# Row-wise sums of squares on ScalarE, r on POOL, and key stores on ScalarE's queue, in a diffusion block's first projections

## The chip, the cores and the metric

The kernel runs on one core of a Trainium2 chip. The metric is the device time of one execution in microseconds (us). The engines are TensorE (PE in the profile, PEld for its weight loads), VectorE (DVE), ScalarE (ACT), GpSimd (POOL) and SyncE (SP), which only issues DMAs here. DMAs go out from an engine's own queue: SP's, or ScalarE's.

## The reference

One layer of a block over 2048 latent tokens and 256 context tokens of width 1024. Tokens are normalised, scaled and shifted, projected, mixed, and projected back:

```
r     = rsqrt(mean(x*x, axis=-1) + 1e-6)
h     = x * r * norm_g * (1 + scale) + shift      # scale, shift from silu(c) @ w_ada
q,k,v,gate (two groups of heads) = h @ w_in       # h for latent and for context tokens
y     = neighbourhood attention (+ context keys), two-way retention
out   = rmsnorm(x + gate * (concat(y) @ w_out)) * final_g
```

The change is in the first line, in the order of the work that makes h, and in the queue of one kind of store.

## The kernel before, in words

All matmuls run on 32-bit data split into a high and a low part, three products for each (high by high, low by high, high by low). Tokens come in nine groups of 256: groups 0 to 7 are latent, group 8 is context. Two groups make a block of 512 tokens.

**Making h.** x is loaded transposed (features on partitions) as `raw[i]`, two halves u of four rows of 128 features. For one group i the acts are:
- `sq` (`squares`): ScalarE squares both halves into `st` tiles; POOL (half 0) and VectorE (half 1) add the feature rows, VectorE joins them (L198 to L203).
- `cs` (`colsum`): TensorE sums over the partitions with a column of ones (L209).
- `rs` (`rstd`, `spread_copy`): VectorE makes mean plus eps, POOL takes the power -0.5, VectorE copies r into a 128 by 256 tile (L214, L215, L220).
- `sp` (`spread`): TensorE multiplies that copy with the identity, so r stands along the columns (L227).
- `mu`: VectorE multiplies half u by r (L241). `ab`: VectorE and ScalarE apply scale and shift (L272, L274). `hl`: ScalarE casts the high part, VectorE or POOL subtracts to get the low part (L279, L283).
- `p`: for groups 0 and 1, scale, shift and split of one feature row k (L262 to L265).
- `s`, `m`, `ar`, `af`: the products with w_ada, the copy of their row, and its transposes (L298 to L332). `x` loads a group, `blk` takes buffers.

**The order.** Nothing is scheduled automatically: each engine runs its instructions in the order in which the program emits them. Five key windows, b = 0 to 4, run over the four blocks of latent tokens and the context; each has 32 steps of three matmuls (L363), numbered n = 0 to 159. In window 0 the four units (128 key columns each) are interleaved, later they follow one another. After step n, `run_acts` emits the acts that `PLAN` lists for n (-1 is ahead of window 0). When a unit is done, ScalarE casts it out of PSUM into an `o` tile, VectorE subtracts (L383, L384) and the tile is stored to `kS` through `store`, on the queue `env["queue"]`. There are two `o` buffers and four `st` buffers. `spill_step` stores finished h to `hS` on SP's queue, for later stages.

**Later stages.** The remaining projections (L374, L671) start after window 4, with weights that are loaded to `st`, cast and split (L345, L347); attention, retention and the output projection follow and are not touched.

Of the kernel before, what the change touches and what calls it, by code (L numbers as in the profile page):

```python
# [9 lines left out]
F32 = mybir.dt.float32  # L10
BF16 = mybir.dt.bfloat16
F32R = mybir.dt.float32r
AF = mybir.ActivationFunctionType
# [5 lines left out]
P = 128  # L19
# [39 lines left out]
]  # L59
# [23 lines left out]
def hybrid_kernel(ctx: ExitStack, tc: tile.TileContext, a: dict, out: bass.AP):  # L83
# [46 lines left out]
    KH = KC // 2  # L130
    env = dict(pp=pool(psx, "pp", 6, space=PSUM), st=pool(sx, "st", 4, side="right"), queue=nc.sync)

# [59 lines left out]
    sqs, rms, rbs, prs = {}, {}, {}, {}  # L192

    def squares(i):
        sqs[i] = []
        for u in range(2):
            sq = xsq[i][u] if i < 2 else env["st"].tile([P, KH, 256], F32, name="st")
            nc.scalar.activation(sq, raw[i][u], AF.Square)  # L198
            eng = (nc.gpsimd, nc.vector)[u]
            eng.tensor_tensor(sq[:, 0:2, :], sq[:, 0:2, :], sq[:, 2:4, :], ALU.add)  # L200
            eng.tensor_tensor(sq[:, 0, :], sq[:, 0, :], sq[:, 1, :], ALU.add)
            sqs[i].append(sq)
        nc.vector.tensor_tensor(sqs[i][0][:, 0, :], sqs[i][0][:, 0, :], sqs[i][1][:, 0, :], ALU.add)  # L203

    def colsum(*ii):
        pm = ptile(None if ii[0] < 4 else psm)
        for j, i in enumerate(ii):
# [4 lines left out]
    def rstd(i):  # L212
        r = env["st"].tile([P, 2], F32, name="rs", bufs=4)
        nc.vector.tensor_scalar(r, rms[i], 1.0 / D, EPS, ALU.mult, ALU.add)  # L214
        nc.gpsimd.tensor_tensor(r, r, mhalf[:, 0:2], ALU.pow)  # L215
        rbs[i] = r

    def spread_copy(i):
        rbs[i, 1] = env["st"].tile([P, 2, P], F32, name="t0", bufs=2)
        nc.vector.tensor_copy(rbs[i, 1], rbs[i].unsqueeze(2).to_broadcast([P, 2, P]))  # L220

# [94 lines left out]
    def ada_row(u):  # L316
        rows[u] = op.tile([P, 2, 512], F32, name="o")[:, 0, :]
        n = 4 if SPL[u] else 2
        (nc.scalar.copy, nc.vector.tensor_copy)[u % 2](rows[u][0:n, :], aps[u][0:n, :])

# [144 lines left out]
    for name, *args in LOADS:  # L465
        lds[name](*args)
    acts = dict(sq=squares, cs=lambda *i: colsum(*i), rs=lambda i: (rstd(i), spread_copy(i)), sp=lambda *i: spread(*i),
                mu=lambda i, u: spread_mul(i, (u,)), ab=prep_ab, hl=prep_hl, blk=alloc_blk, x=load_x, w=lambda: wr.append(w_raw(2560)),
# [22 lines left out]
    def window(b):  # L491
        units = [u_k(w01, 512 + 256 * g, ct, b) for g in range(2) for ct in range(2)]
        left = [KC] * 4
        for n, u in enumerate(STEPS if b == 0 else [u for u in range(4) for _ in range(KC)]):
            if b == 4 and n == 0:
                env["queue"] = nc.scalar
            if b == 4 and n % 8 == 0:
# [1127 lines left out]
```

## Time and profile before

| | before |
|---|---|
| median of 3 runs | 1355.98 us (1355.51 to 1357.14) |
| profiled execution | 1356.78 us, of which 1354.9 us are its span |
| mean granted TensorE clock | 0.995 |
| TensorE, VectorE, ScalarE, POOL busy | 97%, 62%, 45%, 43% |
| DMA traffic | 287.26 MB, mean 212 GB/s |

The span runs from the first to the last instruction. A timeline row reads: start, duration, engine, line, operation, out<-in, shapes, count, and in brackets the idle time before it and what ended that. A row of several instructions gives their joint duration. A wait row reads: who waited for whom, us in total, times, longest. In a row of stretches the last three numbers are granted clock, share of the DMA engines that was busy, and GB/s.

### The profile page before, as it was taken

What the parts mean: (1) busy time and instruction counts of PE and PEld (TensorE: products, weight loads), DVE (VectorE), ACT (ScalarE), POOL (GpSimd) and SP (SyncE); (2) the same over time, 40 slices, a digit from 0 to 9 for tenths busy, and PEclk for the clock granted to TensorE, in tenths of its full rate; (3) what the DMA queues carried; (4) which work ended last, traced back from release to release, by engine and by line L of the source; (5) the groups of instructions that cost most, each with busy time, mean ns of one, the idle gap of its engine ahead of it and who ended that gap; (6) DMA issues with size and microseconds to landing.
All of it is one profiled execution on the core that took longest, in us unless ns stands there. A gap on an engine that the chain in (4) does not pass through costs nothing.

```text
span 1354.9 us, 23100 instructions
## 1 busy us (share of the span) xinstructions
PE 1308.3 (97%) x8236; PEld 1148.7 (85%) x8236; DVE 835.2 (62%) x1444; ACT 606.3 (45%) x1259; POOL 579.0 (43%) x569
## 2 busy tenths in 40 slices
PE   6989999999999999999999999999999999999997
PEld 2467899878898888998899889889999789888885
DVE  5786356776666754377767777776654734444445
ACT  5454333243533344455555465556643244333432
POOL 5452102545104664345535474655523164544442
PEclk9999999999999999999999999999999999999999
DMA  9386788564966657967487887766528888445443
GB/s 363 135 279 233 264 293 224 183 220 154 337 184 209 210 188 238 254 199 210 144 225 203 231 225 205 194 181 193 167 86 294 282 300 273 160 156 171 163 134 117
DMA packets 172086, 287.26 MB, mean 212 GB/s; under 512 B 17345, under 2 KB 92225, under 8 KB 170690
## 3 DMA queue, kind: packets, MB, share of 16 engines
q1 hardware_dynamic: 139554, 228.35, 55.5%
q10 hardware_dynamic: 32416, 57.42, 11.8%
q8 instruction: 66, 1.08, 0.3%
q14 instruction: 50, 0.41, 0.1%
HBM read 194.48 MB, written 91.23 MB: 211 GB/s over the span
## 4 chain that ended last, share of the span: by engine, by line
PE 69%; DMA 9%; DVE 7%; POOL 5%; issue 5%; ACT 3%; SPq 1%; ACTq 0%; POOLq 0%; DVEq 0%
PE mm L374 19%; PE mm L1466 11%; PE mm L671 10%; PE mm L363 7%; PE sS L1028 4%; PE tr L1055 3%; PE po L1076 3%; PE mm L1190 2%; PE tr L1057 2%; PE po L1078 2%; DMA st<-in_w_in_dram 2%; DMA kS<-o 1%; DMA v<-rvS 1%; POOL hlo L531 1%; PE mm L1378 1%
## 5 line engine op out<-in xcount | busy, mean ns | idle before, releaser
L374 PE MATMUL mm<-whi,hlo 128*128 128x256 f32 x832 | 229.2, 283 | 2.0 <-DVE hlo L531 2.0
L374 PE MATMUL mm<-whi,hhi 128*128 128x256 f32 x768 | 224.9, 293 | 0.0
L374 PE MATMUL mm<-wlo,hhi 128*128 128x256 f32 x768 | 217.7, 283 | 0.6 <-DVE wlo L347 0.6
L1059 ACT CAST pt<-tr 128x640 fp32r<-128x640 f32 (+1 forms) x128 | 95.6, 747 | 160.8 <-PE tr L1057 158.3
L1065 DVE TENSOR_TENSOR pt<-tr,pt 128x640 fp32r<-128x640 f32 (+1 forms) x128 | 113.9, 890 | 78.2 <-ACT pt L1059 76.9
L374 PEld LDWEIGHTS mm<-whi,hlo 128*128 128x128 f32 x832 | 157.2, 192 | 2.6 <-DVE hlo L531 2.5
L1048 POOL TENSOR_SCALAR sp<-sp,stt 128x640 f32<-128x640 f32 (+2 forms) x128 | 103.2, 809 | 106.4 <-DVE stt L1047 76.0
L374 PEld LDWEIGHTS mm<-wlo,hhi 128*128 128x128 f32 x768 | 146.8, 191 | 0.8 <-DVE wlo L347 0.8
L374 PEld LDWEIGHTS mm<-whi,hhi 128*128 128x128 f32 x768 | 147.1, 191 | 0.1
L625 POOL TENSOR_TENSOR whi<-st,whi 128x512 fp32r<-128x512 f32 x48 | 64.7, 1369 | 163.1 <-ACT whi L624 163.1
L1037 DVE CUSTOM_DVE_ANT_0 sp<-sS,nb 128x640 f32<-128x640 f32 (+2 forms) x128 | 105.5, 824 | 35.7 <-POOL wlo L347 22.9
L1042 ACT ACTIVATE sp<-sp,stt 128x640 f32<-128x640 f32 (+2 forms) x128 | 107.5, 839 | 20.2 <-DVE stt L1037 19.1
L363 PE MATMUL mm<-hlo,whi 128*128 128x512 f32 x256 | 101.7, 397 | 7.3 <-DVE hlo L283 2.3
L363 PE MATMUL mm<-hhi,whi 128*128 128x512 f32 x256 | 108.0, 422 | 0.0
L1028 PE MATMUL sS<-k,q 128*128 128x256 f32 (+3 forms) x512 | 99.3, 316 | 6.4 <-DVE stt L1037 6.2
L363 PE MATMUL mm<-hhi,wlo 128*128 128x512 f32 x256 | 101.7, 397 | 0.3 <-DVE wlo L347 0.3
L671 PE MATMUL mm<-hhi,whi 128*128 128x512 f32 x336 | 97.4, 394 | 0.0
L1466 PE MATMUL mm<-wor,y 128*128 128x512 f32 x384 | 95.7, 398 | 1.2 <-DVE xt L1475 0.9
L1475 DVE TENSOR_TENSOR xt<-mm,xt 128x512 f32<-128x512 f32 x64 | 43.8, 686 | 82.7 <-PE mm L1466 82.6
L1028 PEld LDWEIGHTS sS<-k,q 128*128 128x128 f32 x512 | 82.8, 188 | 13.7 <-DVE stt L1037 9.9
L1466 PE MATMUL mm<-won,y 128*128 128x512 f32 x336 | 89.9, 406 | 0.0
L1466 PEld LDWEIGHTS mm<-wor,y 128*128 128x128 f32 x384 | 69.9, 188 | 17.4 <-issue 3.5
(258 smaller groups left out, 3037.6 us busy)
## 6 DMA issues: line engine op xcount, KB each, us to landing
st<-in_w_in_dram SPq DMA_DIRECT2D x64, 512.0 KB
q<-qS SPq DMA_DIRECT2D x64, 256.0 KB
hlo<-hS SPq DMA_DIRECT2D x20, 512.0 KB
k<-kS SPq DMA_DIRECT2D x16, 576.0 KB
kS<-o SPq DMA_DIRECT2D x16, 512.0 KB
vB<-o SPq DMA_DIRECT2D x64, 128.0 KB
qS<-o ACTq DMA_DIRECT2D x16, 512.0 KB
woS<-g ACTq DMA_DIRECT2D x32, 256.0 KB
```

The costliest lines, as they stand in the source:

```text
L363: nc.tensor.matmul(pm[:, :n], ww[:, k, cs], h[:, k, :], start=(k == 0 and i == 0), stop=(k == KC - 1 and i == 2))
L374: nc.tensor.matmul(pm[:, t * WG:(t + 1) * WG], h[:, k, o:o + P], ww[:, k, :], start=(k == 0 and i == 0), stop=(k == KC - 1 and i == 2))
L625: nc.gpsimd.tensor_tensor(t[:, 1], r, f(t)[:, 0], ALU.subtract)
L671: nc.tensor.matmul(pm, ww[:, k, :], hh[:, k, :], start=(k == 0 and i == 0), stop=(k == KH - 1 and i == 2))
L1028: nc.tensor.matmul(o, hd["q"][i][:, hl, j * P:(j + 1) * P], k, start=(hl == 0), stop=(hl == 1))
L1037: nc.vector.tensor_tensor_reduce(T["sp"][:, :n], T["s"], nbz[big][:, o:o + n], -1.0, 3e38, ALU.add, ALU.min, T["st"][:, 0:1])
L1042: nc.scalar.activation(sp[:, :n], sp[:, :n], AF.Exp, bias=st[:, 0:1], scale=-1.0, accum_out=st[:, 1:2])
L1048: nc.gpsimd.tensor_scalar(sp[:, :n], sp[:, :n], st[:, 2:3], 0.0, ALU.mult, ALU.add)
L1059: nc.scalar.copy(pt[:, :ng_ + 2, 0, :], tr[:, :ng_ + 2, :])
L1065: nc.vector.tensor_tensor(pt[:, :n, 1, :], tr[:, :n, :], f(pt)[:, :n, 0, :], ALU.subtract)
L1466: nc.tensor.matmul(pm, yy[:, k, :], ww[:, k, sl], start=(k == 0 and i == 0), stop=(k == 3 and i == 2))
L1475: nc.vector.tensor_tensor(xts[t][:, sl], pm, xts[t][:, sl], ALU.add)
```

## The change

For groups 2 to 8, x is loaded a second time, untransposed (tokens on partitions, act `xt`, two tiles of 128 tokens), and ScalarE squares a tile in place and sums along its row in the same instruction (`accum_out`). The adds on POOL and VectorE and TensorE's column sums of these groups are gone. POOL makes mean plus eps, the power and the copy. The row copy of modulation column 2 moves from ScalarE to VectorE. Key stores are issued on ScalarE's queue from the first window on, instead of from window 4. `PLAN` is written anew up to window 2.

```diff
 PLAN = [
...
-    (4, 's', 2, 0), (4, 'x', 4), (4, 'p', 2), (5, 'sq', 2), (7, 'm', 2, 0), (8, 'm', 2, 1), (9, 'p', 3),
+    (4, 's', 2, 0), (4, 'x', 4), (4, 'p', 2), (7, 'm', 2, 0), (8, 'm', 2, 1), (9, 'p', 3), (9, 'sq', 2), (9, 'sq', 3),
...
+    (16, 'af', 3), (16, 'xt', 7), (17, 'p', 7), (17, 'rs', 4), (18, 'p', 6), (18, 'hl', 3, 0), (18, 'mu', 3, 1),
...
-    env = dict(pp=pool(psx, "pp", 6, space=PSUM), st=pool(sx, "st", 4, side="right"), queue=nc.sync)
+    env = dict(pp=pool(psx, "pp", 6, space=PSUM), st=pool(sx, "st", 4, side="right"), queue=nc.scalar)
...
+    def load_xt_(i):
+        sqs[i] = []
+        src = a["ctx"] if i == 8 else a["x"][i * 256:(i + 1) * 256, :]
+        for t in range(2):
+            xt = env["st"].tile([P, KH, 256], F32, name="st").rearrange("p k t -> p (k t)")
+            nc.sync.dma_start(xt, src[t * P:(t + 1) * P, :])
+            sqs[i].append(xt)
+
     def squares(i):
+        if i >= 2:
+            rms[i] = env["st"].tile([P, 2], F32, name="rs", bufs=4)
+            for t, xt in enumerate(sqs[i]):
+                nc.scalar.activation(xt, xt, AF.Square, accum_out=rms[i][:, t:t + 1])
+            return
...
     def rstd(i):
-        r = env["st"].tile([P, 2], F32, name="rs", bufs=4)
-        nc.vector.tensor_scalar(r, rms[i], 1.0 / D, EPS, ALU.mult, ALU.add)
+        r = rms[i] if i >= 2 else env["st"].tile([P, 2], F32, name="rs", bufs=4)
+        (nc.gpsimd if i >= 2 else nc.vector).tensor_scalar(r, rms[i], 1.0 / D, EPS, ALU.mult, ALU.add)
         nc.gpsimd.tensor_tensor(r, r, mhalf[:, 0:2], ALU.pow)
...
-        nc.vector.tensor_copy(rbs[i, 1], rbs[i].unsqueeze(2).to_broadcast([P, 2, P]))
+        (nc.gpsimd if i >= 2 else nc.vector).tensor_copy(rbs[i, 1], rbs[i].unsqueeze(2).to_broadcast([P, 2, P]))
...
-        (nc.scalar.copy, nc.vector.tensor_copy)[u % 2](rows[u][0:n, :], aps[u][0:n, :])
+        (nc.scalar.copy, nc.vector.tensor_copy)[u > 0](rows[u][0:n, :], aps[u][0:n, :])
...
-            if b == 4 and n == 0:
-                env["queue"] = nc.scalar
```

New lines shift the numbers: L265 is L278 in the changed kernel, L272 is L285, L279 is L292, L283 is L296, L383 is L396 and L384 is L397; L151 is the store's line in both.

The order on POOL around step 23 of window 0. Before (L200 and L201 add squares, L215 is the power, L265 a low part of `p`, L283 a low part of `hl`):

```order
L200 TENSOR_TENSOR st<-st 128x512
L201 TENSOR_TENSOR st<-st 128x256
L215 TENSOR_TENSOR rs<-rs,mhalf 128x2 x2
L265 TENSOR_TENSOR hlo<-hhi 128x256 x3
L215 TENSOR_TENSOR rs<-rs,mhalf 128x2
L283 TENSOR_TENSOR hlo<-hlo,hhi 128x4x256 x2
```

POOL at the same place now (L227, L228 and L233 are mean plus eps, power and copy of r, here of groups 4 and 5):

```order
L296 TENSOR_TENSOR hlo<-hlo,hhi 128x4x256
L278 TENSOR_TENSOR hlo<-hhi 128x256 x2
L227 TENSOR_SCALAR rs<-rs 128x2
L228 TENSOR_TENSOR rs<-rs,mhalf 128x2
L233 COPY t_501<-rs 128x256
L278 TENSOR_TENSOR hlo<-hhi 128x256
L227 TENSOR_SCALAR rs<-rs 128x2
L228 TENSOR_TENSOR rs<-rs,mhalf 128x2
L233 COPY t_531<-rs 128x256
L296 TENSOR_TENSOR hlo<-hlo,hhi 128x4x256
```

The first low part of group 2 has moved ahead of the last three low parts of `p`, and r of group 4 stands between them.

ScalarE from the end of window 0 to the casts of groups 4 and 5, before (L383 casts a unit, L198 squares, L274 scales, L279 casts a half group):

```order
L383 CAST o<-mm 128x512
L198 ACTIVATE st<-hhi 128x1024 x2
L383 CAST o<-mm 128x512
L274 ACTIVATE hhi<-hhi,mods 128x256 x2
L383 CAST o<-mm 128x512 x2
L274 ACTIVATE hhi<-hhi,mods 128x256 x2
L198 ACTIVATE st<-chi 128x1024 x2
L274 ACTIVATE hhi<-hhi,mods 128x256
L279 CAST hhi<-hhi 128x4x256 x3
```

ScalarE at the same place now (from the third unit of window 0 on; L206 squares with a row sum, L151 issues a key store):

```order
L396 CAST o<-mm 128x512
L151 DMA kS_64<-o 256x1x512
L206 ACTIVATE st,rs<-st 128x1024 x2
L396 CAST o<-mm 128x512
L151 DMA kS_61<-o 256x1x512
L287 ACTIVATE hhi<-hhi,mods 128x256 x2
L206 ACTIVATE st,rs<-st 128x1024 x2
L396 CAST o<-mm 128x512
L151 DMA kS_61<-o 256x1x512
L287 ACTIVATE hhi<-hhi,mods 128x256 x2
L396 CAST o<-mm 128x512
L151 DMA kS_62<-o 256x1x512
```

Behind every cast of a unit now stands the issue of its store, which waits for VectorE's subtraction; the squares that follow are those of later groups.

More of the change, by code (lines that the diff above doesn't have):

```diff
@@ L192, in hybrid_kernel @@
     sqs, rms, rbs, prs = {}, {}, {}, {}
-    def squares(i):
+    def load_xt_(i):
[5 more added lines that the diff above has]
+            sqs[i].append(xt)
+    def squares(i):
+        if i >= 2:
[3 more added lines that the diff above has]
+            return
         sqs[i] = []
         for u in range(2):
-            sq = xsq[i][u] if i < 2 else env["st"].tile([P, KH, 256], F32, name="st")
+            sq = xsq[i][u]
             nc.scalar.activation(sq, raw[i][u], AF.Square)
@@ L205, in colsum @@
     def colsum(*ii):
-        pm = ptile(None if ii[0] < 4 else psm)
+        pm = ptile()
         for j, i in enumerate(ii):
@@ L466, in hybrid_kernel @@
         lds[name](*args)
-    acts = dict(sq=squares, cs=lambda *i: colsum(*i), rs=lambda i: (rstd(i), spread_copy(i)), sp=lambda *i: spread(*i),
+    acts = dict(sq=squares, xt=load_xt_, cs=lambda *i: colsum(*i), rs=lambda i: (rstd(i), spread_copy(i)), sp=lambda *i: spread(*i),
                 mu=lambda i, u: spread_mul(i, (u,)), ab=prep_ab, hl=prep_hl, blk=alloc_blk, x=load_x, w=lambda: wr.append(w_raw(2560)),
```

29 rows, old and new, of the table PLAN are left out of this document.

## The prediction

> **What bounds the kernel now.** I read the page's first lines, then what TensorE waits for up to 240 us, then that stretch's granted clock and DMA share, then the timelines of the engines around each wait.
>
> ```profile
> span 1354.9 us, 23100 instructions
> PE 1308.3 (97%) x8236; PEld 1148.7 (85%) x8236; DVE 835.2 (62%) x1444; ACT 606.3 (45%) x1259; POOL 579.0 (43%) x569
> PE mm L311 <- ACT o L298: 10.3, 1, 10.3
> ...
> PE mm L374 <- DVE wlo L347: 1.3, 2, 0.7
> ```
>
> TensorE is busy 97% of the span, so only its waits and its own work can be won. The change touches the windows of keys and what prepares their activations. Of TensorE's waits up to 240 us, the 10.3 us at the start are untouched. The others, 9.6 us with the rows below, are for low parts of activations (L283, L265), for a spread of r (L227) and for low parts of weights (1.3 us, L347):
>
> ```profile
> 37.85 0.50 PE L363 MATMUL mm<-hlo,whi 128*128 128x512 f32 x1 [1.72 <-DVE hlo L265]
> 59.03 1.38 PE L227 MATMUL mm<-ident,t 128*128 128x128 f32 x8
> 65.12 0.47 PE L363 MATMUL mm<-hlo,whi 128*128 128x512 f32 x1 [0.37 <-DVE hlo L265]
> 74.40 0.47 PE L363 MATMUL mm<-hlo,whi 128*128 128x512 f32 x1 [1.96 <-DVE hlo L283]
> 77.75 0.47 PE L363 MATMUL mm<-hlo,whi 128*128 128x512 f32 x1 [0.38 <-DVE hlo L283]
> 100.83 0.49 PE L363 MATMUL mm<-hlo,whi 128*128 128x512 f32 x1 [2.32 <-POOL hlo L283]
> 104.03 0.50 PE L363 MATMUL mm<-hlo,whi 128*128 128x512 f32 x1
> 106.27 0.88 PE L227 MATMUL mm<-ident,t 128*128 128x128 f32 x4 [1.51 <-DVE t L220]
> ...
> 107.37 0.63 PE L363 MATMUL mm<-hlo,whi 128*128 128x512 f32 x1
> 107.80 0.63 PE L363 MATMUL mm<-hhi,wlo 128*128 128x512 f32 x1
> 104.00:108.00 4.00, 2.47 (x9) 1.84 (x10) 3.04 (x6) 1.10 (x2) 2.67 (x3) 0.84 0.61 208
> ```
>
> Each step n of a window is three matmuls of 0.23 us, 0.69 us. 65.12 is step 23, 74.40 and 77.75 steps 32 and 36, 100.83 and 104.03 steps 64 and 68. After the two waits around 100 and 106 the clock reads 0.84 (last but two columns), and six matmuls come 0.43 us apart instead of 0.23: 1.2 us more.
>
> **What is taken away.** The column sums are seven groups' small matmuls:
>
> ```profile
> 51.87 0.79 PE mm L209 x8
> 109.70 0.58 PE mm L209 x4
> 124.87 0.34 PE mm L209 x4
> 35.49 1.37 DVE L263 TENSOR_SCALAR hhi<-hhi,mods 128x256 f32<-128x256 f32 x1
> 36.90 0.90 DVE L265 TENSOR_TENSOR hlo<-hhi 128x256 fp32r<-128x256 f32 x1
> 28.41 0.40 DVE L263 TENSOR_SCALAR hhi<-hhi,mods 128x256 f32<-128x256 f32 x1
> 35.24 1.47 POOL L200 TENSOR_TENSOR st<-st 128x512 f32<-128x512 f32 x1
> ```
>
> Groups 2 and 3 cost 0.79, group 7 (at the slow clock) 0.58, the other four 0.34 each: 2.7 us of TensorE's own time go (-2.7). The adds of squares on POOL also hold up VectorE: the scaling at 35.49 took 1.37 us beside a POOL add, alone it takes 0.40, and the subtraction behind it took 0.90 where half is usual. TensorE's wait at 37.85 hangs on these two, so 1.4 of its 1.72 us go (-1.4). r of groups 6 and 7 is ready long before its spread, so the wait of 1.51 goes (-1.5).
>
> **Loads.** Fourteen loads of 512 KB (7.3 MB) are added on SP's queue.
>
> ```profile
> 50.00:60.00 10.00, 10.00 (x41) 4.76 (x40) 7.84 (x17) 2.67 (x5) 5.13 (x6) 1.00 0.00 1
> 31.93 4.10 SPq L190 DMA_DIRECT2D hhi<-in_xT_dram  x4
> SPq L151 <- DVE o L384: 79.6, 14, 33.3
> ```
>
> The DMA engines stand idle there (0.00 in the last column but one) because SP, after 36 us, waits 33.3 us at the first key store. Six of the seven groups' loads go into that hole. The first four take the places at 31.93 that groups 4 and 5 had; those then come some 5 us later and are needed only at step 26. Cost: nothing, since the hole covers it; without it a load would cost about 1 us, what each of the four at 31.93 took to get into the full queue. The copy of row 2 of the modulation moves from ScalarE to VectorE, which then has nothing else ready: nothing.
>
> **Step 23, a new wait.** Spread 2 and 3 come at step 14 instead of 16. With the savings, two steps and four transposes less before them they start near 55 us (59.03 before). VectorE then does two multiplications (1.2 us each) and four scalings (0.35), and ScalarE casts group 2 by 60.0. POOL does, in this order, group 2's first low part, two of p 7, r of group 4, and only then the low part of p 6 that step 23 needs.
>
> ```profile
> 60.45 1.22 DVE L241 TENSOR_TENSOR hlo<-hlo,mm 128x1024 f32<-128x1024 f32 x1 [0.53 <-PE mm L227]
> 69.59 2.41 POOL L283 TENSOR_TENSOR hlo<-hlo,hhi 128x1024 fp32r<-128x1024 f32 x1 [0.86 <-ACT hhi L279]
> 70.22 2.90 DVE L272 TENSOR_SCALAR hlo<-hlo,mods 128x256 f32<-128x256 f32 x4
> L215 POOL TENSOR_TENSOR rs<-rs,mhalf 128x2 f32<-128x2 f32 x9 | 6.4, 706 | 26.7 <-DVE rs L214 26.7
> L265 POOL TENSOR_TENSOR hlo<-hhi 128x256 fp32r<-128x256 f32 x8 | 6.3, 804 | 9.0 <-DVE hhi L263 9.0
> L1383 POOL TENSOR_SCALAR rss<-rss 128x4 f32<-128x4 f32 x16 | 3.1, 194 | 70.8 <-ACT rjk L1382 70.8
> L887 POOL MEMSET nb<- 128x256 f32 x4 | 1.1, 311 | 0.0
> ```
>
> r on POOL: 0.19 + 0.71 + the copy. No row shows that copy; it lies between the memset of 256 (0.31) and a subtraction of 256 (0.80). I take 0.4, as it has one operand: 1.3 us. From 60.0: 2.4 + 2 x 0.8 + 1.3 + 0.8 is 66.1, and VectorE's scalings of p 7, locked out beside the first POOL row as at 70.22 (four in 2.90, one alone 0.40), push it to about 66.5. TensorE arrives near 62.6 (65.12 less the old wait, 1.4 and 0.8): a wait of 3.9 where 0.37 stood (+3.5). Bounds: +1.3 if POOL and VectorE fall apart luckily, +5 if r is cut up by VectorE's work. In return groups 2 and 3 are split long before steps 32 and 36: 1.96 + 0.38 go (-2.3).
>
> **The stores on ScalarE.** Sixteen key stores leave SP's queue for ScalarE's. Each now holds ScalarE until VectorE's subtraction is done, then for the issue:
>
> ```profile
> L383 ACT CAST o<-mm 128x512 fp32r<-128x512 f32 x16 | 9.3, 583 | 32.5 <-PE mm L363 24.1 <-DMA kS<-o 7.4 <-DVE hhi L241 0.9
> 69.62 0.69 DVE L384 TENSOR_TENSOR o<-mm,o 128x512 fp32r<-128x512 f32 x1
> 155.51 0.60 ACTq L151 DMA_DIRECT2D kS<-o  x1
> 74.88 7.29 DMA kS<-o
> 83.61 3.71 DMA kS<-o
> 155.51 9.03 DMA kS<-o
> 88.90 2.00 ACT L198 ACTIVATE st<-chi 128x1024 f32<-128x1024 f32 x2
> 98.51 3.07 DVE L272 TENSOR_SCALAR hhi<-hhi,mods 128x256 f32<-128x256 f32 x3
> ```
>
> 0.58 + 0.69 + 0.6 is some 1.8 us for each unit. Behind them queue the squares and the casts that window 2 needs. From about 72.8 us, when group 3 is cast, to group 5's first cast ScalarE has six units (10.8), four squares (4.0), five scalings of 256 columns (a cast of 512 takes 0.58, so some 0.5 each: 2.5), three casts as long as a square (3.0), and the third unit's wait for the first store to land (two o buffers). Landing took 3.71 to 9.03; 3.71 is nearest, since the hole has cleared the loads away: 1.9 us beyond the unit between. The sum is 22.2: group 5 is cast at 95. POOL has group 4's low part first, from 94: 2.4 + 2.4, and 0.9 for what VectorE holds it up, is 99.7 (100.83 before). TensorE would arrive at 96.5 (98.5 before, less 1.4, 1.8 of sums and 2.3, plus 3.5): a wait of 3.2 instead of 2.3 (+0.9). Step 68 needs group 5's second half: VectorE's three scalings (3.07 beside POOL at 98.51), a subtraction, a store, group 8's two squares, a cast, a subtraction. If the scalings pass between POOL's two rows they end near 98.4; then 0.7 + 0.6 + 2.0 + 1.0 + 1.2 and half a us of hand-overs give 104.4. Behind the second row it is 106.7. I take 104.4, as the row at 70.22 shows them blocked once and then running through: 1.9 of wait against 0.3 (+1.6). The clock falls in both kernels: 0.
>
> Later SP is free of stores: the reloads that were issued at 153.76, just ahead of the 9.03 us store, go out some 3 us sooner, so the weight casts behind that store come in time: up to -1.3 (the L374 waits), at worst 0. I take -1.3, since their cause is named.
>
> **Sum.** -2.7 - 1.4 - 1.5 + 3.5 - 2.3 + 0.9 + 1.6 - 1.3 = -3.2. The profiled execution took 1356.78 (span 1354.9), 0.8 above the median of 1355.98; carried over to the median: 1352.8. Later stages start earlier by the same.
>
> **The clock, by rule and by row.** In the rows the clock fell after waits of 2.32 and 1.51 us some 4 us apart, and not after 1.96 alone. By them it falls once here too, around steps 64 and 68, which is the 0 above; a fall after step 23 costs nothing, since TensorE then arrives at step 64 1.2 us later and waits so much less. The Trainium skill ("TensorE: Matmul & The Clock Gate", Part 1) puts the fall to half rate at an idle window of about 3.4 us. By that rule step 23 falls and step 64 stands at the edge; no trace here has a wait of that length after the start. A second slow stretch, between steps 64 and 96, is a rival below.
>
> **Rivals.**
> - Slower: the store lands late. Place: the third unit's cast on ScalarE, at 77 us. Each us beyond 3.7 moves window 2 by one; beyond about 6 the sixth unit waits too. At 7.29 it costs 4.6 (1357.4), at 9.03 some 8 (1360.8). It decides from about 8 us on. For it: the 9.03 us store already stood on ScalarE's queue. Against: loads were in flight then, which here have gone before.
> - No change: VectorE's scalings fall behind POOL's second row at step 68: +2.3, 1355.1. A second slow stretch costs 1.2 as the first did: 1354.0. A landing at 7.29 gives 1357.4.
> - Faster still: ScalarE and POOL keep pace, steps 64 and 68 wait no longer than before and the clock holds: -2.7 - 1.2 more, 1348.9.
>
> **How the numbers follow.** About 0.2% (2.7 us) is what a measurement tells from no change. Forecast (-2.7 to -5) 0.28, faster still 0.17: faster 0.45. Same 0.34 (the scalings 0.16, the clock 0.08, landing 0.10). Slower 0.21 (landing 0.14, a longer step 23 with both window 2 waits 0.07). Range 1347.8 to 1360.0, which leaves out late landings near 9 us; the forecast's own is 1350.5 to 1353.3.
>
> **What would show it.** L209 only before 20 us; a wait of 3 to 5 us for POOL at step 23; none at steps 32 and 36; step 64 near 99.7, step 68 near 104.4, no wait at spread 6; the L374 waits gone; kS on ScalarE's queue landing in about 4 us. It is wrong if ScalarE's third cast waits over 5 us for kS, or if step 23 does not wait.

## The result: slower by 0.5%, and the profile after

The changed kernel took 1364.56 us in the median of 4 executions (1362.48 to 1367.29), the kernel before 1356.03 (1355.51 to 1357.14). The ratio is 1.0053, 95% interval 1.0038 to 1.0068: some 7 us slower. The prediction, 1352.8, was wrong, and its range (to 1360.0) did not hold the time. The profiled execution of the changed kernel took 1364.89, its span is 1363.1.

The first lines of the page after, and the longest of TensorE's waits from 20 to 300 us (the one at the start, 10.2 us, is that of before):

```profile
span 1363.1 us, 23048 instructions
PE 1311.6 (96%) x8208; PEld 1151.1 (84%) x8208; DVE 816.6 (60%) x1410; ACT 607.2 (45%) x1272; POOL 565.5 (41%) x569
PE mm L376 <- POOL hlo L278: 4.6, 2, 4.2
PE mm L387 <- ACT whi L358: 3.0, 1, 3.0
PE mm L376 <- ACT hhi L292: 2.0, 1, 2.0
PE mm L376 <- POOL hlo L296: 1.9, 1, 1.9
PE mm L376 <- DVE hlo L296: 1.4, 2, 0.8
PE mm L376 <- ACT hhi L275: 1.2, 1, 1.2
```

TensorE has 28 instructions fewer but is busy 3.3 us longer, and it waits in other places. Its timeline shows where; L376 is what L363 was, L387 what L374 was, L240 the spread that was L227:

```profile
63.95 0.50 PE L376 MATMUL mm<-hhi,whi 128*128 128x512 f32 x1 [1.19 <-ACT hhi L275]
68.68 0.79 PE L376 MATMUL mm<-hlo,whi 128*128 128x512 f32 x1 [4.23 <-POOL hlo L278]
102.45 0.50 PE L376 MATMUL mm<-hlo,whi 128*128 128x512 f32 x1 [1.92 <-POOL hlo L296]
107.25 0.51 PE L376 MATMUL mm<-hhi,whi 128*128 128x512 f32 x1 [1.96 <-ACT hhi L292]
108.50 0.62 PE L376 MATMUL mm<-hlo,whi 128*128 128x512 f32 x1 [0.75 <-DVE hlo L296]
109.35 1.06 PE L240 MATMUL mm<-ident,t 128*128 128x128 f32 x4
168.94 0.39 PE L387 MATMUL mm<-whi,chi 128*128 128x256 f32 x1 [2.98 <-ACT whi L358]
170.20 0.58 PE L387 MATMUL mm<-wlo,chi 128*128 128x256 f32 x1 [0.76 <-DVE wlo L360]
```

The rows are steps 23 (two), 64, 68 (two), the spread of group 6, and the first unit behind window 4. Against before:

| low part or first matmul | before | after | difference | forecast |
|---|---|---|---|---|
| step 64 | 100.83 | 102.45 | +1.6 | -1.1 |
| step 68 | 104.03 | 108.50 | +4.5 | +0.4 |
| spread of group 6 | 106.27 | 109.35 | +3.1 | -1.1 |
| first product of the next stage (L671, now L682) | 233.9 | 240.7 | +6.8 | -3.2 |
| span | 1354.9 | 1363.1 | +8.2 | -3.2 |

The second thing that is new is the clock. Stretches of the changed kernel; the last three numbers are granted clock, DMA share and GB/s, the first after the length is how long TensorE was busy:

```profile
64.36:67.78 3.42, 0.09 (x1) 0.00 (x0) 3.38 (x6) 1.47 (x3) 3.18 (x5) 1.00 0.98 327
67.78:71.19 3.41, 2.51 (x6) 2.03 (x7) 2.33 (x5) 2.34 (x4) 2.59 (x6) 0.50 1.04 382
71.19:74.60 3.41, 3.41 (x11) 2.83 (x11) 2.74 (x2) 1.12 (x2) 2.13 (x1) 0.50 1.09 385
105.32:108.73 3.41, 0.73 (x2) 0.41 (x3) 1.50 (x2) 2.35 (x4) 0.89 (x2) 1.00 0.45 165
108.73:112.14 3.41, 3.41 (x11) 2.82 (x11) 0.32 (x1) 0.00 (x0) 0.40 (x1) 0.50 0.42 156
166.76:170.17 3.41, 0.50 (x2) 0.30 (x2) 1.67 (x3) 2.29 (x4) 0.00 (x0) 1.00 0.24 80
170.17:173.59 3.42, 3.39 (x16) 3.39 (x17) 1.87 (x3) 0.37 (x1) 0.00 (x0) 0.50 0.62 157
```

Behind each of the three new waits the clock stands at exactly half, for 6.8, 3.4 and 3.4 us. In the kernel before there is one such stretch up to 300 us (106.7 to 110.1). Behind these waits the matmuls of a step come 0.43 us apart instead of 0.23, so 13.7 us at half clock are some 6.8 us of TensorE's time, against 1.7 before, as far as no later wait hides them.

### The profile page after: what moved, and what is told of

Same layout as the page of the kernel before. It is cut to its first block, busy times and chain, and to the rows that moved or that the text cites. A ratio compares the mean times of both kernels' runs of the same rounds, so it can differ in the third digit from the quotient of the medians.

```text
span 1363.1 us, 23048 instructions
## 1 busy us (share of the span) xinstructions
PE 1311.6 (96%) x8208; PEld 1151.1 (84%) x8208; DVE 816.6 (60%) x1410; ACT 607.2 (45%) x1272; POOL 565.5 (41%) x569
## 4 chain that ended last, share of the span: by engine, by line
PE 68%; DVE 6%; DMA 5%; POOL 5%; issue 4%; ACT 3%; ACTq 0%; SPq 0%; POOLq 0%; DVEq 0%
PE mm L387 21%; PE mm L1477 11%; PE mm L682 10%; PE mm L376 5%; PE sS L1039 5%; PE tr L1066 3%; PE po L1087 3%; PE mm L1201 2%; PE tr L1068 2%; PE po L1089 2%; DMA v<-rvS 1%; PE mm L1389 1%; PE mm L1388 1%; PE mm L1387 1%; POOL hlo L542 1%
## 5 line engine op out<-in xcount | busy, mean ns | idle before, releaser
L387 PE MATMUL mm<-whi,hlo 128*128 128x256 f32 x832 | 228.9, 283 | 1.6 <-DVE hlo L542 1.6
L387 PE MATMUL mm<-whi,hhi 128*128 128x256 f32 x768 | 224.5, 292 | 0.0
L387 PE MATMUL mm<-wlo,hhi 128*128 128x256 f32 x768 | 217.2, 283 | 0.0
L387 PEld LDWEIGHTS mm<-whi,hlo 128*128 128x128 f32 x832 | 156.5, 191 | 2.6 <-DVE hlo L542 2.6
L387 PEld LDWEIGHTS mm<-whi,hhi 128*128 128x128 f32 x768 | 146.5, 191 | 0.1
L387 PEld LDWEIGHTS mm<-wlo,hhi 128*128 128x128 f32 x768 | 146.2, 190 | 0.0
L376 PE MATMUL mm<-hhi,whi 128*128 128x512 f32 x256 | 109.1, 426 | 3.1 <-ACT hhi L292 2.0
L376 PE MATMUL mm<-hlo,whi 128*128 128x512 f32 x256 | 103.0, 402 | 8.2 <-POOL hlo L278 4.6
L376 PE MATMUL mm<-hhi,wlo 128*128 128x512 f32 x256 | 102.8, 402 | 0.3 <-DVE wlo L360 0.3
L682 PE MATMUL mm<-hhi,whi 128*128 128x512 f32 x336 | 97.4, 394 | 0.0
```

What stands on the lines that cost most here:

```text
L376: nc.tensor.matmul(pm[:, :n], ww[:, k, cs], h[:, k, :], start=(k == 0 and i == 0), stop=(k == KC - 1 and i == 2))
L387: nc.tensor.matmul(pm[:, t * WG:(t + 1) * WG], h[:, k, o:o + P], ww[:, k, :], start=(k == 0 and i == 0), stop=(k == KC - 1 and i == 2))
L682: nc.tensor.matmul(pm, ww[:, k, :], hh[:, k, :], start=(k == 0 and i == 0), stop=(k == KH - 1 and i == 2))
```

## The experiments

Eighteen kernels were run in five sets, each against the kernel before on the same chip. A median alone says little: executions of one kernel lie up to 11 us apart, and before's own median moved between 1355.5 and 1357.0. So the ratio to before counts; its interval is 0.0010 to 0.0024 to each side (1.4 to 3.3 us).

| kernel | ratio to before, 95% interval |
|---|---|
| changed kernel | 1.0053 (1.0038 to 1.0068) |
| 1 before, key stores on ScalarE | 1.0140 (1.0127 to 1.0153) |
| 2 changed, key stores on SP | 1.0056 (1.0043 to 1.0070) |
| 3 r of group 4 behind p 6 | 1.0033 (1.0020 to 1.0046) |
| 4 group 8's first cast at step 118 | 1.0021 (1.0005 to 1.0036) |
| 5 group 8's squares behind group 5's last cast | 1.0029 (1.0018 to 1.0041) |
| 6 group 2's split behind p 7 and p 6 too | 1.0053 (1.0035 to 1.0071) |
| 7 changed, TensorE filled | 1.0036 (1.0023 to 1.0049) |
| 8 mended: 3, 4 and 5 | 1.0013 (1.0001 to 1.0026) |
| 9 mended, group 4 split early | 1.0014 (0.9998 to 1.0030) |
| 10 mended, key stores on SP | 1.0049 (1.0035 to 1.0064) |
| 11 changed, group 4 split early | 1.0068 (1.0050 to 1.0085) |
| 12 mended with 6 and 9 | 1.0022 (1.0008 to 1.0035) |
| 13 mended, TensorE filled | 0.9992 (0.9981 to 1.0004) |
| 14 mended, group 7's squares late | 1.0085 (1.0061 to 1.0109) |
| 15 the same, filled | 1.0048 (1.0030 to 1.0066) |
| 16 as 14, loads of groups 7 and 8 late | 1.0051 (1.0034 to 1.0068) |
| 17 the same, filled | 1.0015 (1.0004 to 1.0025) |
| 18 before, filled | 0.9998 (0.9987 to 1.0009) |

**1 and 2: the two halves of the change.** The first theory was that ScalarE, held by each key store, makes the loss.

```diff
 # 1: before
-... queue=nc.sync)
+... queue=nc.scalar)
 # 2: the changed kernel
-... queue=nc.scalar)
+... queue=nc.sync)
+            if b == 4 and n == 0:
+                env["queue"] = nc.scalar
```

> The kernel before, with nothing changed but the queue of the sixteen key stores of windows 0 to 3 (ScalarE's from the start). Theory (ScalarE, held by each key store until VectorE's subtraction is done and then for the 0.52 us issue, is late with the casts of groups 4, 5 and 8): slower than before by 3 to 6 us, 1359 to 1362, with longer waits at steps 64 or 68 than the 2.32 of before, and a wait for whi in window 4 as in the changed kernel (2.98 us there). Rival (the row-wise sums on ScalarE and POOL, with 7.3 MB more to load, cost the time): within 1.5 us of before, 1354.5 to 1357.5.

> The changed kernel, with the key stores of windows 0 to 3 on SP's queue again (the row-wise sums alone). Theory (the stores on ScalarE are the loss): 1352 to 1357, a gain of 7 to 12 us over the changed kernel; the wait for whi in window 4 (2.98 us) is gone or under 1 us, step 64 is reached before 100.8 us. Rival (the sums and their loads are the loss): 1361 to 1365, hardly faster than the changed kernel.

The stores alone cost 19 us, far more than expected. The two longest of TensorE's waits there:

```profile
PE mm L209 <- DVE st L203: 8.2, 3, 3.5
PE mm L374 <- ACT whi L345: 4.0, 1, 4.0
```

The squares queue behind the stores on ScalarE, and TensorE's column sums wait for them; the change takes these sums away. But the sums alone, with the stores on SP (kernel 2), are as slow as both together, so the theory fell. There, step 68 waits for another reason; ScalarE, then TensorE:

```profile
105.72 1.06 ACT L206 ACTIVATE st<-st 128x1024 f32<-128x1024 f32 x1 [5.63 <-DMA st<-in_ctx_dram]
109.13 0.79 PE L376 MATMUL mm<-hhi,whi 128*128 128x512 f32 x1 [2.88 <-ACT hhi L292]
```

Group 8's loads queue behind the key stores on SP, ScalarE waits for them, and the cast that step 68 needs stands behind these squares. Each half of the change is bad without the other; what kernel 2 and the changed kernel share is the place of group 8's squares.

**4 and 5: two places in the order.** ScalarE, VectorE and POOL of the changed kernel around step 68:

```profile
97.03 5.36 POOL L296 TENSOR_TENSOR hlo<-hhi 128x1024 fp32r<-128x1024 f32 x2 [6.30 <-ACT hhi L292]
97.70 5.17 DVE L285 TENSOR_SCALAR hhi<-hhi,mods 128x256 f32<-128x256 f32 x3
104.07 1.06 ACT L206 ACTIVATE st<-st 128x1024 f32<-128x1024 f32 x1 [3.64 <-DMA hS<-hhi]
106.17 1.03 ACT L292 CAST hhi<-hhi 128x1024 fp32r<-128x1024 f32 x1
```

VectorE's scalings end at 102.87, the squares run from 104.07, and the cast for step 68 only at 106.17. And around window 4 (ScalarE, POOL, SP twice, ScalarE twice; L527 reloads h):

```profile
150.84 1.05 ACT L292 CAST chi<-st 128x1024 fp32r<-128x1024 f32 x1 [1.32 <-DVE o L397]
151.97 2.39 POOL L296 TENSOR_TENSOR clo<-st,chi 128x1024 fp32r<-128x1024 f32 x1 [7.10 <-ACT chi L292]
129.74 24.98 SPq L176 DMA_DIRECT2D st<-in_w_in_dram  x4
154.81 2.14 SPq L527 DMA_DIRECT2D hhi<-hS  x4
155.90 0.56 ACTq L151 DMA_DIRECT2D kS<-o  x1
166.42 0.37 ACT L396 CAST o<-mm 128x256 fp32r<-128x256 f32 x1 [8.60 <-DMA kS<-o]
```

Group 8's last half is cast behind a key store, POOL's low part ends at 154.4, and only then are the `st` buffers free for which SP's weight loads have waited. They go out with the reloads right ahead of the key store of 155.90, and ScalarE waits for that to land until 166.4; the weight cast TensorE needs stands behind. In the kernel before, the same store, the last of window 3, went out on SP's queue ahead of the reloads:

```profile
153.14 0.53 SPq L151 DMA_DIRECT2D kS<-o  x1
153.76 2.43 SPq L516 DMA_DIRECT2D hhi<-hS  x4
```

```diff
 # 4
-    (117, 'ab', 8, 0), (127, 'hl', 8, 0), (127, 'w2'),
+    (117, 'ab', 8, 0), (118, 'hl', 8, 0), (118, 'w2'),
 # 5
-    (60, 'sq', 8), (61, 'hl', 5, 1),
+    (61, 'hl', 5, 1), (61, 'sq', 8),
```

> The changed kernel, with the cast of group 8's first half and the weight load behind it at step 118, ahead of the key cast and store of that unit on ScalarE, not at step 127 behind them. Theory (the store holds that cast back from 147 to 150.84 us; so POOL's low part ends at 154.4 and the weight loads, which wait for its buffers, go out at 154.7, together with the reloads, right ahead of the key store that then takes 10.44 us to land and keeps whi and TensorE waiting): POOL's low part ends near 150.5, the weight loads go out by 151, the wait for whi (2.98 us) falls below 1 us, and the time falls by 2.5 to 4 us, to 1360.5 to 1362. Rival (the store's landing is slow because ScalarE's queue shares the engines with any loads in flight): the landing stays near 10 us, and the time within 1 us of 1364.6.

> The changed kernel, with group 8's squares on ScalarE behind the cast of group 5's second half, not ahead of it. Theory (the squares, 104.07 to 106.2 us, hold the cast back by 2.1 us, so step 68 waits 1.96 and 0.75 us and the clock is at half rate from 108.7 us): the cast starts near 104.1, the two waits at step 68 fall to at most 1 us together, spread 8 comes 1.5 to 2.5 us earlier, and the time is 1361 to 1363. Rival (what step 68 gives is waited for at steps 96 or in window 4, where ScalarE and POOL are late on their own account): the time stays within 1 us of 1364.6 and the whi wait of 2.98 us grows.

Both did what was expected at their places, and 4 gained a little more. In 4, POOL ends at 149.0 and TensorE's wait for whi there is 0.42 instead of 2.98 us; in 5, there is no wait at step 68 and the spread of group 6 stands at 107.37. The ratios fall by 0.0032 and 0.0024 (4.3 and 3.3 us); 4's interval lies clear of the changed kernel's, 5's just overlaps it.

**3 and 6: step 23.**

```diff
 # 3
-(17, 'p', 7), (17, 'rs', 4), (18, 'p', 6),
+(17, 'p', 7), (18, 'p', 6), (18, 'rs', 4),
 # 6: as 3, and
-(14, 'ab', 3, 0), (14, 'hl', 2, 0), (15, 'mu', 2, 1),
+(14, 'ab', 3, 0), (15, 'mu', 2, 1),        # hl 2,0 now behind p 6
```

> The changed kernel, with r of group 4 on POOL behind the low part of p 6, not ahead of it. Both theories: TensorE's wait at step 23 (4.23 us) falls by about 1.8 us, to 2.4. Theory (the wait at step 64 hangs on ScalarE's and POOL's chain of casts and not on TensorE's arrival, so it takes up what step 23 gives): the time stays within 1 us of the changed kernel's 1364.6, and the wait at step 64 (1.92 us) grows by about 1.8. Rival (waits add up): 1362.8 or less, with the wait at step 64 unchanged.

> The changed kernel, with group 2's first cast and low part (and r of group 4) behind p 7 and p 6 on ScalarE and POOL, so that step 23 has nothing on POOL ahead of it but its own low parts. Both theories: the waits at step 23 (1.19 and 4.23 us) fall to 2.5 us or less together, and the 6.8 us at half clock behind them go. Theory (step 64 hangs on the chain of casts, which TensorE's arrival does not set): step 64 stays within 1 us of 102.45, its wait grows from 1.92 to 4 or 5 us, and the time within 1.5 us of 1364.6. Rival (waits and slow stretches add up): 1360 to 1362, step 64 some 3 us earlier.

TensorE in 6, at step 23 and step 64:

```profile
64.72 0.77 PE L376 MATMUL mm<-hlo,whi 128*128 128x512 f32 x1 [1.46 <-DVE hlo L278]
101.88 0.79 PE L376 MATMUL mm<-hlo,whi 128*128 128x512 f32 x1 [3.95 <-POOL hlo L296]
```

Step 23 comes 4 us earlier, step 64 0.6, and the time is that of the changed kernel within the intervals: what step 23 gives, step 64 takes. In kernel 3 the wait at step 64 grew from 1.92 to 3.27 us, as its theory said, yet it seems to gain 2.7 us, as its rival said; its interval overlaps that of the changed kernel, and its trace shows no place that would explain the gain.

**7, 13 and 18: the clock by itself.** Matmuls that nothing reads stand ahead of the steps where TensorE waits, fewer than fill the wait. They bring no data earlier.

```diff
+    def fill_pe(n):
+        pm, h = ptile(psm), blk[0][0]
+        for _ in range(n):
+            nc.tensor.matmul(pm, h[:, 0, 0:P], h[:, 0, :], start=True, stop=True)
 # 7: ahead of steps 23, 64, 68: 18, 6, 8; behind window 4: 12. 13: ahead of 23 and 64: 18, 14.
 # 18: ahead of step 64 and of the spread of group 6: 9, 6
```

> The changed kernel, with matmuls that nothing reads put where TensorE waits: 18 ahead of step 23, 6 ahead of step 64, 8 ahead of step 68, 12 ahead of the first unit after window 4 (0.23 us each, 4.1, 1.4, 1.8 and 2.8 us, less than the waits there). They don't shorten a wait for data; they only keep TensorE busy. Theory (a stretch of 3.41 us in which TensorE stands idle for about half or more is followed by one or two of 3.41 us at half clock; here at 67.8, 108.7 and 170.2 us): no half clock at these three places, and of the 3.4 + 1.7 + 1.7 us lost there the last two come back, the first being hidden by the wait at step 64: 1360.5 to 1362.5. Rival (the half clock is not set by idling, or its cost is hidden everywhere): the half clock is seen there as before, or the time within 1 us of 1364.6.

In 7 the half clock at 67.8, 108.7 and 170.2 us is gone, but TensorE still waits 2.42 us at step 64, and the clock falls at 101.5 for 3.4 us. The ratio falls by 0.0017 (2.3 us; the intervals overlap). Kernel 8 makes the three edits of order at once:

> The changed kernel with three edits of order: r of group 4 behind p 6 on POOL, group 8's squares behind the cast of group 5's second half, group 8's first cast and the weight load behind it at step 118. Theory (places add up where they lie behind one another: step 68 2 to 2.7 us, window 4 some 4, the half clock of each): no wait over 1 us between step 68 and 190 us, spread 8 near 130, the first unit after window 4 near 163.5, and the time 1354 to 1358, level with before. Rival (each edit uncovers the next wait): 1359 or more.

It reaches 1.0013, 5.4 us below the changed kernel; TensorE waits nowhere over 1 us between step 68 and 190 us. The three edits one by one gave 2.7, 4.3 and 3.3 us; that they give less together than the sum of 10.3 is not explained, and each figure can be off by 2 us or more. Kernel 13 fills it:

> The mended kernel (r of group 4 behind p 6, group 8's squares behind group 5's last cast, group 8's first cast at step 118; 1358.3), with 18 matmuls that nothing reads ahead of step 23 and 14 ahead of step 64 (0.23 us each, less than the waits of 5.1 and 3.7 us there). Theory (what is left between the mended kernel and before is the clock, at half rate from 64.9 for 6.8 us, hidden, and from 102.4 for 3.4 us): no half clock at 102, the time 1 to 2.5 us below the mended kernel, 1356 to 1357.3. Rival (the rest lies elsewhere, or the half clock is not set by idling): within 0.7 us of 1358.3, or half clock at 102 all the same.

The same stretch behind step 64 in kernel 8 and in kernel 13:

```profile
102.44:105.85 3.41, 3.41 (x10) 2.64 (x9) 1.74 (x3) 2.21 (x4) 0.00 (x0) 0.50 0.99 354
```

```profile
102.40:105.80 3.40, 3.21 (x12) 2.18 (x12) 1.72 (x4) 1.76 (x2) 0.00 (x0) 1.00 1.03 361
```

Step 64 stands at 102.03 in the one and 102.42 in the other, so the data were no earlier; the ratio falls by 0.0021, 2.9 us (the intervals just overlap), and is level with before. One stretch of 3.41 us at half clock is worth 1.7 us at most, so the 2.9 are more than the one stretch that this trace shows. The whole of its clock agrees: one minus the mean granted clock, times the time, is 8.9 us on the mean of kernel 8's executions and 4.0 of kernel 13's (11.3 for the changed kernel, 4.8 to 6.9 for before in the five sets; 2 to 4 of each lie behind the last work). That the clock held in this one execution is partly luck: kernel 13 still waits 2.70 us at step 64, and in 7 it fell behind 2.42.

> The kernel before, with 9 idle matmuls ahead of step 64 and 6 ahead of the spread of r of group 6 (2.1 and 1.4 us, less than the waits of 2.32 and 1.51 us there). Theory (the half clock that follows such waits is a cost of its own, in every kernel): the half clock at 106.7 us is gone, and the time 1 to 2 us below before, 1354 to 1355. Rival (in the kernel before these waits seldom bring the clock down, and it was so by chance in the profiled execution): within 0.7 us of before.

In the kernel before the fill gained nothing (0.9998). The half clock at 106.7 is gone, but it fell at 75.3, behind the unfilled wait of 1.96 at step 32. So shorter waits bring the clock down in some executions only; the rival held there, as far as an interval that reaches 1.8 us below before can tell.

**9, 11 and 12: what sets step 64?** It stayed near 102 whatever was done at step 23. One suspect was that POOL has two low parts in a row there.

```diff
-(42, 'ab', 4, 1),
+(42, 'ab', 4, 1), (42, 'blk', 2), (42, 'hl', 4, 0), (43, 'hl', 4, 1),
-(53, 'blk', 2), ... (55, 'hl', 4, 1), (55, 'hl', 4, 0), (55, 'hl', 5, 0),
+... (55, 'hl', 5, 0),
```

> The changed kernel with the three edits of order of the last mended kernel (1358.3), and group 4's two casts and low parts at step 42, right behind its scalings, not at step 55 beside group 5's. Theory (step 64 is set by ScalarE's three casts in a row from 95 us and POOL's two low parts of 2.4 us behind them, 5.3 us in which VectorE's scalings stand still): only group 5's low part is left on POOL there, from about 98 to 100.4 us; step 64 falls from 102.0 to 100 to 101, its wait from 3.7 to about 2, and the time to 1354.5 to 1357. Rival (the two casts only put off the key casts and stores behind them on ScalarE, and group 5 with them): step 64 at 101.5 or later, 1358 or more.

> The changed kernel with group 4's two casts and low parts at step 42 alone. Theory (as for the kernel with all four edits, but group 8's squares still stand ahead of group 5's last cast, and window 4 is as it was): step 64 at 100 to 101 instead of 102.45, step 68 at most 1 us earlier, the time 1362.5 to 1364. Rival (step 64 is the one place that counts, all later ones follow it): the time falls by the whole 2 us and more, to 1361 to 1362.5.

> The kernel with all four edits of order, and group 2's first cast and low part behind p 7 and p 6 as well, which took the waits at step 23 from 5.4 to 2.8 us and changed nothing in the time while step 64 waited. Theory (what step 23 gives is taken up by step 64 only as far as that waits): with step 64 ready near 100.5, TensorE arrives near 95 and waits all the same; within 1 us of the kernel with the four edits alone. Rival (the chain of casts itself starts earlier when TensorE ends its first units earlier): 1.5 to 3 us below it.

All three missed: step 64 at 102.35, 103.00 and 103.38. The early casts only put off the key casts and stores behind them, as the rival said: in 9, the scalings of group 5's second half start at 99.90 us, and in kernel 8 at 97.32. Kernel 12 agrees with 9 within the intervals: step 23 is absorbed once more.

**10: the stores again, in the mended order.**

> The mended kernel (r of group 4 behind p 6, group 8's squares behind group 5's last cast, group 8's first cast at step 118; 1358.3) with the key stores of windows 0 to 3 on SP's queue again. Theory (the stores on ScalarE are no loss of their own once nothing urgent is queued behind them; what lost with the stores on SP were group 8's squares, whose loads arrived at 105.7, ahead of the cast for step 68): the wait of 2.9 us at step 68 is gone, 1356.5 to 1360. Rival (loads that queue behind the stores on SP come late elsewhere too): 1361 or more.

The wait at step 68 is gone, but TensorE waits elsewhere, as the rival said:

```profile
172.32 0.38 PE L387 MATMUL mm<-whi,chi 128*128 128x256 f32 x1 [2.97 <-ACT whi L358]
```

So with the order mended, the key stores on ScalarE's queue are worth 0.0036, 4.9 us. The change's idea was right there, and its order hid it.

**14 to 17: ScalarE's chain.** The second suspect for step 64 were group 7's squares, 2.1 us on ScalarE at 86.7 us.

```diff
 # 14
-(38, 'sq', 7), ... (50, 'xt', 8), (50, 'rs', 7),
+... (61, 'hl', 5, 1), (61, 'sq', 7), (62, 'rs', 7), (62, 'xt', 8), (70, 'sq', 8), (72, 'rs', 8),
 # 16: 'x' 7 and 8 at step 65, 'xt' 8 at 66, 'sq' 8 at 76.  15, 17: 14, 16 with 18 and 7 idle matmuls
```

> The mended kernel with group 7's squares (2.1 us on ScalarE, at 86.7 us) behind group 5's last cast too, and group 8's squares, with their loads, at step 70. Theory (step 64 is set by ScalarE's chain of key casts, stores and squares from 72 us on, which lies 5 us behind TensorE; whatever leaves this chain brings step 64 forward by as much, until TensorE's arrival at 98.3): step 64 at 99.9 to 100.5 instead of 102.0, its wait 1.6 to 2.2 instead of 3.7, step 68 without a wait, the time 1.5 to 3 us below the mended kernel, 1355.3 to 1356.8. Rival (the waits of key casts for the landing of stores, or VectorE and POOL, set step 64): step 64 at 101.5 or later, time within 0.7 us of 1358.3.

> The kernel with group 7's squares moved as well, and 18 idle matmuls ahead of step 23 and 7 ahead of step 64 (1.6 us). Theory (both add up: the chain gives 1.5 to 2 us, the clock 1 to 1.7): 1353.5 to 1355.5, below before. Rival (with the wait at step 64 under 2 us the clock does not fall there anyway): the same as with group 7's squares moved alone, within 0.7 us.

Kernel 14 went the other way: step 64 at 105.64. SP's loads, ScalarE's store and its next cast, and the store's landing from the chain of waits:

```profile
83.14 1.39 SPq L176 DMA_DIRECT2D st<-in_ctxT_dram  x2
84.61 0.86 SPq L190 DMA_DIRECT2D clo<-in_xT_dram  x2
85.38 0.52 ACTq L151 DMA_DIRECT2D kS<-o  x1
95.23 0.59 ACT L396 CAST o<-mm 128x512 fp32r<-128x512 f32 x1 [5.29 <-DMA kS<-o]
85.38 9.77 DMA kS<-o
```

The 2.1 us were saved and 5.3 lost again, to a store that landed behind four loads. Kernel 15 missed with it: the fill brought 1.0085 down to 1.0048, still above before.

> The kernel with group 7's squares behind group 5's last cast (1369.9, the wrong way), with the loads of groups 7 and 8 issued at steps 65 and 66 instead of 46 to 62, so that SP has them behind its spill of group 4. Theory (there the chain on ScalarE lost its 2.1 us of squares and gained a wait of 5.3 us for a key store, issued at 85.4 us right behind four loads of 83.1 to 85.5 and landed at 95.2; without the loads in front it lands within 5 us): no wait over 1 us for the key store at 88 to 95 us, step 64 at 99.9 to 100.5, and the time 1354.5 to 1358. Rival (the landing is long whatever is in flight, or group 7, loaded later, is late for step 96): the wait for the store as before, or a wait of over 2 us at step 96; 1362 or more.

> The same kernel with 18 idle matmuls ahead of step 23 and 7 ahead of step 64. Theory (as with the filled mended kernel, 3 us below the mended one): 1 to 3 us below the kernel without them, 1353 to 1356, below before. Rival: no gain over it.

Kernel 16 without loads in front (ScalarE's next cast there, steps 64 and 96 of TensorE, and ScalarE between them):

```profile
89.55 0.57 ACT L396 CAST o<-mm 128x512 fp32r<-128x512 f32 x1
100.00 0.50 PE L376 MATMUL mm<-hlo,whi 128*128 128x512 f32 x1 [1.38 <-POOL hlo L296]
128.39 0.79 PE L376 MATMUL mm<-hhi,whi 128*128 128x512 f32 x1 [3.82 <-ACT hhi L292]
115.85 1.05 ACT L292 CAST hhi<-chi 128x1024 fp32r<-128x1024 f32 x1 [4.99 <-DMA hS<-chi]
```

Now no key cast waits for a store between 80 and 100 us, and step 64 stands at 100.00, as expected: it is ScalarE's chain of key casts, stores and squares, and the landing of the stores in it, that set step 64. But the time is 1.0051, since group 6's cast waits 5 us for a spill and step 96 3.8 us: half of the theory and the rival's second half both held. Filled (17) it is 1.0015, 4.9 us less, and here the intervals lie apart; the data came hardly earlier (step 64 at 99.85, step 96 at 127.63), and the clock's loss fell from 11.6 to 6.7 us on the mean of the executions. This is the clearest sign in these runs that the half clock is a cost of its own. Below before, as was expected, it did not get. A kernel that also clears step 96 was not tried, nor one with a third `o` buffer. No version beat the kernel before.

## Why the prediction was wrong

By its own steps:

- **Column sums, the wait at 37.85, steps 32 and 36, the spread of group 6** came as predicted: no L209 beyond 20 us, 0.27 us of wait left at 37.36, none at the others. The copy of r on POOL took 0.40 us alone, as assumed, and 0.77 in the one ahead of step 23. The reading "where half is usual" was too kind: of VectorE's eight subtractions of this kind before, one took 0.43 us and the others 0.83 to 1.41.
- **"Step 23, a new wait"** was right in kind and short in size: 1.19 and 4.23 us, 3.9 were forecast. Group 2 was cast by 61.7, not by 60.0, and r took 1.9 us on POOL (66.01 to 67.94), not 1.3. Kernels 6 and 12 show no cost of it beyond the intervals, because step 64 waits anyway; the prediction had said so of the slow clock behind it.
- **Step 64, "group 5 is cast at 95"**: it was cast at 97.9, so step 64 came at 102.45 and not at 99.7. Two terms were short. A first unit held ScalarE for 3.9 us (71.73 to 75.61), not 1.8, since VectorE's subtraction stood behind a low part locked out beside POOL (2.54 us from 71.86, where 1.22 is its time alone); and the first store took some 5 us to land (75.03 to 80.14), not 3.71. That is 2.1 and 1.4 us more; ScalarE began 1.1 earlier than the 72.8 of the sum. Kernels 14 and 16 show the landing as the lever: 5.6 us at step 64 between them. ScalarE's casts of the first and third unit, the first store, and the casts of groups 4 and 5:

```profile
71.73 0.57 ACT L396 CAST o<-mm 128x512 fp32r<-128x512 f32 x1
75.03 0.58 ACTq L151 DMA_DIRECT2D kS<-o  x1
80.14 0.59 ACT L396 CAST o<-mm 128x512 fp32r<-128x512 f32 x1 [3.43 <-DMA kS<-o]
94.97 2.94 ACT L292 CAST hhi<-hhi 128x1024 fp32r<-128x1024 f32 x3
```

- **Step 68, "if the scalings pass between POOL's two rows they end near 98.4"**: only one passed: the first ended behind POOL's first row (at 100.19), the second behind its second (102.55), and the last at 102.87 (97.70 + 5.17). The rest of the sum (subtraction, store, squares, cast, subtraction) held: 108.50. This was named as the rival for no change, at +2.3; with the later step 64 it came to 4.1 us over the forecast of 104.4. The squares stood in the sum, but not the question whether they had to stand there: kernel 5 takes some 3.3 us back by moving them.
- **"Later SP is free of stores: the reloads go out some 3 us sooner" (-1.3)** was the worst step. They went out at 154.81, 1.05 later than before: SP was free of stores, but it stood at L176 for buffers that POOL frees, and POOL waited for a cast that now stood behind a key store. And the store that now landed late was one that had gone out ahead of the reloads before. Kernel 4 shows it: 4.3 us. Instead of -1.3 the waits there went from 1.3 to 3.7 us, and their half clock came on top.
- **"The clock falls in both kernels: 0"**: it fell for 13.7 us of half clock up to 200 us, not 3.4. The fills price such stretches: 2.9 us from kernel 8 to 13 and 2.3 from the changed kernel to 7, with intervals that overlap, 4.9 from 16 to 17, with intervals apart. "Not after 1.96 alone" did not hold either: in kernel 18 the clock fell behind this same wait. There the whole 1.96 us lay in one stretch of the grid that the last section describes, in the kernel before 1.85. The prediction weighed the Trainium skill ("TensorE: Matmul & The Clock Gate", Part 1) and found that by its idle window of 3.4 us step 23 falls; it did.
- **The loads** cost TensorE nothing that a trace shows by themselves, but "the hole covers it" was half true: where key stores share the engines with them they land 5 us later (kernel 14).

Put together by the start of the next stage: it was forecast near 230.7 us and came at 240.7. By the spread of group 6 the kernel was 4.2 us behind the forecast, the waits behind window 4 add 3.7, and the half clock behind them 1.7, which is 9.6 of the 10.0.

Neither sign of being wrong that the prediction named was seen: ScalarE's third cast waited 3.4 us, not over 5, and step 23 waited. The rival "slower" named ScalarE's wait for a landing store; its mechanism was there, in part at the place named (3.4 us of wait at 80.14) and in full at window 4, where 10.4 us of landing kept ScalarE waiting 8.6. It was given 0.21 with a longer step 23.

What stays open: by the start of the same matmul the profiled execution lies 6.8 us behind before at 240 us, but 3.4 at 1037 us, and 9 again from 1172 us on, with half clock at 1061 and 1160 that before's profiled execution does not have; that one has it at 356, where the changed kernel's does not. These waits exist in both kernels; whether they bring the clock down changes from one execution to the next. So of the 8.2 us between the two spans several are such chance, while the medians, and kernels 4, 5, 8, 16 and 17, carry the account.

## What to carry to other kernels

When a transfer moves to another engine's queue, list what stands behind it in that engine's program order and ask for each what waits for it, two steps on: here a cast held back by a store held back POOL, then SP's loads, then another store's landing, and TensorE waited 20 us later. A saving ahead of a wait that another chain sets is worth nothing until that chain gets shorter, and a chain gets shorter only if the transfers in it land as fast as before. Count a wait of 2 us or more on TensorE as possibly 1.7 us dearer for each 3.41 us of half clock behind it that no later wait hides; filling such waits was worth 2 to 5 us here, and nothing that could be measured in the kernel before, whose waits are 2.3 us and less.

## What the runs showed of the hardware

- The half clock comes in stretches of 3.41 us or multiples, on a fixed grid: 67.78, 108.73 and 170.17 lie 12 and 18 times 3.413 us apart. The stretch ahead of each had TensorE idle for 3.33, 2.68 and 2.91 of its 3.41 us. Less was enough: in the 19 traces that have half clock from 20 to 240 us, it followed every stretch of the grid with 1.96 us idle or more, while of those with 1.49 to 1.85 some were followed by it (1.64 before, from 103.27; 1.49 in kernel 4, from 188.1) and some not (1.72 and 1.85 before, from 35.00 and 72.55). The Trainium skill (the same page and part) tells of a free-running window of this length, and the trace agrees; that the window need not be idle as a whole is what the trace adds. Where the grid lies differs between the profiled executions, so the same wait can cost differently. That this is why kernel 8's executions reach from 1354.06 to 1361.62 is likely, but not shown.
- Three VectorE scalings took 5.17 us beside two POOL low parts of 5.36 in a row, and 5.11 to 5.16 in eight of the other kernels. VectorE got in between with one scaling only. The second rows of POOL and VectorE:

```profile
100.00 2.39 POOL L296 TENSOR_TENSOR hlo<-hhi 128x1024 fp32r<-128x1024 f32 x1
100.11 2.44 DVE L285 TENSOR_SCALAR hhi<-hhi,mods 128x256 f32<-128x256 f32 x1
```

  The first scaling had taken 2.49 us from 97.70, this one takes 2.44, the third 0.40. The Trainium skill ("SBUF — State Buffer", "SBUF: two separate sides") calls the shared ports an exclusive lock that the loser waits for; the trace agrees.
- A key store of 512 KB took some 5 us to land with no loads right ahead of it (75.03 to 80.14) and 9.8 to 10.4 behind four or more loads of 512 KB on another queue (kernel 14 from 85.38; the changed kernel from 155.90).
